# Where the gain and bias of the mixers' norms are applied, and what the residual and the MLP's sums then read

## The chip, the cores and the metric

One core of one Trainium2 chip runs the whole program in one launch. The metric is the device time of one execution in microseconds (us); the time of the kernel before is the median of three runs. A profile is one further execution, recorded by the hardware profiler.

## The reference

A decoder trunk of two layers on 1024 tokens of width 1024, all in float32. Layer 0 mixes tokens with a gated convolution, layer 1 with windowed attention. Around each mixer and each MLP stands a residual sum and a layer norm; a gated embedding of the token closes each layer:

```
x = layer_norm(ALPHA * x + mixer(x), mix_g, mix_b)        # the change is here
x = layer_norm(ALPHA * x + square(relu(x @ w_up)) @ w_down, mlp_g, mlp_b)
x = x + (p @ w_proj) * sigmoid(x @ w_gate)
layer_norm(x, g, b) = (x - mean(x)) * rsqrt(var(x) + 1e-5) * g + b
```

g and b are vectors over the 1024 features. The first norm's result is read twice: by the MLP's up product, which needs it transposed (features on the partitions), and by the residual of the second sum, which needs it with tokens on the partitions.

## The kernel before, in words

**Numbers.** Every float32 operand of a product is split into a high part (a cast to fp32r, by ScalarE, `xh`, `wh`) and a low part (value minus high, by VectorE, `xl`, `wl`); a product is three matmuls, high by high, high by low, low by high (`mm3`). All large products are done block-wise with seven instead of eight sub-products, for which sums and differences of the quarters of each operand are formed. For the up product the token side is cut into four quarters: features 0 to 511 or 512 to 1023 (q) by tokens 0 to 511 or 512 to 1023 (h), kept as `self.xT[q, h]`, each a high and a low tile of 128 x 4 x 512.

**Order of work.** The program is written as a list of operations; a planner (`Recorder.schedule`) simulates the engines with fixed costs, and issues each engine's instructions in the order that it finds. `nc.later(n)` lowers the priority of what stands in it by n places, `nc.slack` makes the planner take an operand as ready some ns later. `nc.either` leaves it to the planner whether VectorE or GpSimd (POOL) runs an instruction. Engines run in that order, strictly one after another. All instructions are issued from one line, L488, so that the profile is read by tiles and not by lines. Every DMA is issued by SP, in one queue.

**Buffers.** Tiles come from tagged slots in the order of the requests: `z` (4), `g` (4), `t` (5), `A` (9), `B` (8), `X` (8), `E` (4 double ones), `bo` (2), `v` (1), `cst` (1). PSUM has eight banks, which move between the tags `ps` (sums of products) and `tr` (transposes).

**The end of a mixer.** `mix_out` (layer 0) and `outputs` in `attention` (layer 1) multiply by the output weights, a group of token tiles at a time. `mixed` adds the residual on VectorE. When both halves of a tile of 128 tokens are done, `layer_norm` runs on it: `stats` (VectorE and three small instructions on POOL and VectorE), then for each half of 512 features a normalization on ScalarE (`z`), a multiplication by a row of g on VectorE and an addition of a row of b on VectorE or POOL. g and b are rows of 512 loaded to all partitions (tag `g`). `to_xT` transposes the result on TensorE, four 128 x 128 blocks to a bank, and splits the bank into `self.xT`: a cast by ScalarE and a subtraction by VectorE that read PSUM. The tile itself is stored to DRAM (`self.mid`), from where `residual` loads it late in the down product and multiplies it by ALPHA.

**The MLP's start.** `mlp` first runs the top-left products of five pairs of up columns (`EARLY`; 24 matmuls each), which need only quarters (0, 0) and (1, 0). Meanwhile `token_forms` builds the four sums from all quarters. Where only high and low parts are at hand, it adds both parts of each quarter: five VectorE instructions for the first two sums of a block of 128 features, three each for the third and the fourth. Then follow the 16 pairs of up columns, seven products of 12 matmuls each; their hidden values are combined by `keep` and stored. In between, `work` prepares weights for later stages.

Of the kernel before, what the change touches and what calls it, by code (L numbers as in the profile page):

```python
# [10 lines left out]
F32 = mybir.dt.float32  # L11
# [65 lines left out]
UP_WORK = {6: ("gate", 0), 10: ("gate", 1), 14: ("gate", 2), 16: ("gate", 3), 20: ("down", 0), 22: ("down", 1)}  # L77
HID_SLACK = 3000.0
# [442 lines left out]
class Emit:  # L521
# [259 lines left out]
    def to_xT(self, xt, t, raw=None, slack=SLACK):  # L781

        for q in range(2):
            pv = self.transpose4(self.blocks(xt[q]), slack).rearrange("p (a b) -> p a b", a=4)
            sl = (slice(None), slice(None), slice(t % 4 * P, (t % 4 + 1) * P))
            if raw and q == 0:
                self.nc.scalar.copy(raw[t // 4][sl], pv)
                if t >= 4:
                    continue
# [23 lines left out]
    def layer_norm(self, t, gb, spill=None, raw=None, sums=None):  # L813
# [3 lines left out]
        rs = self.stats(xt) if sums is None else self.row_stats(xt, sums)  # L817
        for q in range(2):
# [3 lines left out]
            (nc.vector if sums and t % 4 > 1 else nc.either).tensor_tensor(out=xt[q], in0=z, in1=gb[1][q], op=ALU.add)  # L822
        self.to_xT(xt, t, raw, LAST_SLACK[self.gates] if sums else SLACK)
# [27 lines left out]
    def setup(self):  # L851
        nc, d = self.nc, self.d
        cst = self.const("cst", (P, 256 + NT * 32 + 2 * NH), F32)
        self.cc, self.sums = cst[:, 0 : 32 + 64 + TAPS + 1], cst[:, 32 + 64 + TAPS + 1 :]
        self.ident = self.const("ident", (P, P), F32)
        self.mhalf = self.const("mhalf", (P, 32), F32)[:, 0:1]
# [26 lines left out]
    def conv(self):  # L883
# [15 lines left out]
        nc.sync.dma_start(self.ident, d["ident"])  # L899
        scr = {}  # L900
# [385 lines left out]
        with nc.after(exchange):  # L1286
            gb = self.load_row("g", d["mix_g"][0:1]), self.load_row("g", d["mix_b"][0:1])
            ws.add(*[d["w_out"][0, u] for u in range(2)])
            ws.pump()
# [17 lines left out]
        self.mix_out(d["w_out"], gb)  # L1307
# [25 lines left out]
    def mix_out(self, w, gb):  # L1333

        nc, ws = self.nc, self.ws
        self.raw = None
# [97 lines left out]
    def token_forms(self, tags):  # L1434
# [18 lines left out]
        raw = {}  # L1453
        b11r, b12r = [[v[:, k, :] for k in range(4)] for v in self.raw] if self.raw else (None, None)
        sub, add = ALU.subtract, ALU.add
        B = {k: [quarter(k + 4 * j, h) for j in range(2) for h in range(2)] for k in range(4)}

        for k, (b11, b12, b21, b22) in B.items():
            if self.raw:
                t1 = tt(b12r[k], b11r[k], sub, b12r[k])  # L1460
            else:
                t1 = tt(f(b12[0]), f(b11[0]), sub)
                lo = tt(f(b12[1]), f(b11[1]), sub)
                tt(t1, lo, add, t1)
            raw[k] = self.sb(tags[4])
            tt(f(b22[0]), t1, sub, raw[k])
            tt(raw[k], f(b22[1]), add, raw[k])
            for j, r in ((2, raw[k]), (1, t1)):
                forms[j][k] = two(tags[j])
                self.split(r, *forms[j][k])  # L1470
        for k, (b11, b12, b21, b22) in B.items():
            if self.raw:
                t3 = tt(raw[k], b11r[k], sub, b11r[k])
            else:
                t3 = tt(raw[k], f(b11[0]), sub)
                tt(t3, f(b11[1]), sub, t3)
            forms[3][k] = two(tags[3])
            self.split(t3, *forms[3][k])
        for k, (b11, b12, b21, b22) in B.items():
            t4 = tt(f(b21[0]), raw[k], sub)  # L1480
            tt(t4, f(b21[1]), add, t4)
# [4 lines left out]
    def mlp(self, i):  # L1486
# [54 lines left out]
        for f in pairs:  # L1541
# [99 lines left out]
    def down_seven(self, i, cs, start, end, rest):  # L1641
# [41 lines left out]
        def product(a, b, to, bank=None, own=(None, None), last=False, low=None, full=()):  # L1683
# [11 lines left out]
            for t in range(4 if last else 0):  # L1695
                with nc.later(LATE if to == [(0, 1)] else 0):
                    self.layer_norm(t + 4 * to[0][0], gb, None, self.raw, sums[t + 4 * to[0][0]])
# [217 lines left out]
    def attention(self):  # L1915
        nc, d, ws = self.nc, self.d, self.ws
        ac = self.sb("cst", n=256 + NT * 32 + 2 * NH)
# [99 lines left out]
        self.x, self.raw = [], None  # L2017
# [8 lines left out]
        gb = []  # L2026
        held = {}

        def outputs(cc, tiles, end, norm):
# [300 lines left out]
```

## Time and profile before

| | |
|---|---|
| median of 3 runs | 2104.5 us (2100.63 to 2106.58) |
| the profiled execution | 2101.52 us, of which its span is 2099.8 |
| TensorE (PE) busy | 2082.9 us, 99% |
| its weight loads (PEld) | 1729.3 us, 82% |
| VectorE (DVE) busy | 1700.9 us, 81% |
| ScalarE (ACT) busy | 1207.1 us, 57% |
| GpSimd (POOL) busy | 295.1 us, 14% |
| granted TensorE clock | 1.0 |
| end of layer 0's mixer, then its MLP's first products | from about 310 to 430 us |
| the same in layer 1 | from about 1365 to 1490 us |

How to read the rows. A row of the timeline gives the start in us, the time that it took, engine, operation, the tiles out<-in, shape and count, and in brackets the idle time of the engine before it and what ended it. A row of the windows gives the stretch, its length, then the busy time and number of instructions of PE, PEld, DVE, ACT and POOL, the granted clock, the DMA share and GB/s. A row of the groups ends in the busy time and the mean ns of one, then the engine's idle time before them and who ended it. Matmul records overlap each other: one of 512 columns lasts 0.39 us, and its distance to the next tells the rate.

### The profile page before, as it was taken

Reading aid. Unit: us, or ns where it says so; the run is one execution under the profiler, and the core shown is the slowest. Engines: PE = TensorE matmul, PEld = TensorE weight load, DVE = VectorE, ACT = ScalarE, POOL = GpSimd, SP = SyncE. Lnnn points to the kernel's source line nnn. Section 1 sums busy time; section 2 is a strip of 40 time slices with the busy share of each in tenths; the row PEclk is TensorE's granted clock in tenths of the full one; section 3 lists DMA queues with packets and bytes.
Section 4 is the critical chain, followed back from the end, with each engine's and each line's share of the span. In section 5 each row is a group of like instructions: output and inputs, shape, how many; then the busy total and the mean of one; then the engine's idle time right before and its main releaser. Section 6 shows DMA issues by size and latency. Waiting matters only on the chain.

```text
span 2099.8 us, 29286 instructions
## 1 busy us (share of the span) xinstructions
PE 2082.9 (99%) x9784; PEld 1729.3 (82%) x9784; DVE 1700.9 (81%) x2631; ACT 1207.1 (57%) x2224; POOL 295.1 (14%) x513
## 2 busy tenths in 40 slices
PE   9999999999999999999999999999999999999999
PEld 7888888888888888888888888877888888888877
DVE  8999789987876889987963587989787778888688
ACT  6777654766666644345742488656666563333374
POOL 0533114000000000002220265520000000000040
PEclk9999999999999999999999999999999999999999
DMA  6669864878776879875566877587878785575635
GB/s 226 192 202 296 294 197 143 298 265 273 269 270 216 307 257 319 279 262 215 171 211 192 319 227 238 188 298 249 269 259 275 254 285 200 181 247 171 233 126 191
DMA packets 239063, 502.01 MB, mean 239 GB/s; under 512 B 24128, under 2 KB 62784, under 8 KB 238912
## 3 DMA queue, kind: packets, MB, share of 16 engines
q1 hardware_dynamic: 238912, 500.14, 71.2%
q8 instruction: 77, 1.26, 0.2%
q14 instruction: 74, 0.61, 0.1%
HBM read 337.26 MB, written 160.17 MB: 237 GB/s over the span
## 4 chain that ended last, share of the span: by engine, by line
PE 88%; DVE 5%; DMA 3%; ACT 2%; issue 1%; POOL 1%; SPq 0%; DVEq 0%; ACTq 0%; POOLq 0%
PE ps L488 67%; PE tr L488 21%; DVE z L488 1%; DMA wh<-gate_t 1%; ACT z L488 1%; DVE g L488 1%; POOL sm L488 1%; DMA raw<-in_w_up_dram 1%; DVE wl L488 1%; DVE B L488 1%; DVE xl L488 0%; DVE t L488 0%; DVE v L488 0%; DVE sm L488 0%; DVE X L488 0%
## 5 line engine op out<-in xcount | busy, mean ns | idle before, releaser
L488 PE MATMUL ps<-xh,xl 128*128 128x512 f32 x618 | 240.5, 389 | 0.0
L488 PE MATMUL ps<-xl,xh 128*128 128x512 f32 x618 | 240.5, 389 | 0.0
L488 PE MATMUL ps<-xh 128*128 128x512 f32 x618 | 240.5, 389 | 0.0
L488 POOL TENSOR_SCALAR sm<-sm 128x1 f32<-128x1 f32 x72 | 26.8, 374 | 1362.9 <-DVE E L488 1200.1
L488 PE MATMUL ps<-xl,wh 128*128 128x512 f32 x536 | 210.3, 393 | 0.4 <-DVE xl L488 0.4
L488 PE MATMUL ps<-xh,wh 128*128 128x512 f32 x536 | 209.4, 393 | 0.8 <-DVE xl L488 0.5
L488 PE MATMUL ps<-xh,wl 128*128 128x512 f32 x536 | 210.0, 392 | 0.0
L488 ACT CAST wh<-raw 128x1024 fp32r<-128x1024 f32 (+2 forms) x130 | 115.5, 890 | 77.5 <-PE ps L488 47.9
L488 PE MATMUL ps<-wh,xh 128*128 128x512 f32 (+1 forms) x352 | 138.5, 395 | 3.2 <-DMA wh<-gate_t 1.2
L488 PE MATMUL ps<-wh,xl 128*128 128x512 f32 (+1 forms) x352 | 138.6, 394 | 0.1
L488 PE MATMUL ps<-wl,xh 128*128 128x512 f32 (+1 forms) x352 | 138.6, 394 | 0.0
L488 ACT CAST xh<-wh 128x1024 fp32r<-128x1024 f32 x76 | 79.7, 1049 | 99.7 <-PE ps L488 53.0
L488 PEld LDWEIGHTS ps<-xh 128*128 128x128 f32 x618 | 116.0, 188 | 24.2
L488 PEld LDWEIGHTS ps<-xh,xl 128*128 128x128 f32 x618 | 116.0, 188 | 24.1
L488 ACT CAST wh<-g 128x512 fp32r<-128x512 f32 x136 | 81.2, 618 | 94.9 <-PE ps L488 52.6
L488 PEld LDWEIGHTS ps<-xl,xh 128*128 128x128 f32 x618 | 116.1, 188 | 23.9
L488 DVE TENSOR_TENSOR wl<-raw,wh 128x1024 fp32r<-128x1024 f32 (+2 forms) x96 | 93.2, 972 | 37.0 <-ACT wh L488 35.8
L488 DVE TENSOR_TENSOR wl<-g,wh 128x512 fp32r<-128x512 f32 x136 | 90.9, 690 | 38.5 <-ACT wh L488 38.4
L488 PEld LDWEIGHTS ps<-xh,wh 128*128 128x128 f32 x536 | 100.9, 188 | 21.9 <-DVE xl L488 0.7
L488 PEld LDWEIGHTS ps<-xl,wh 128*128 128x128 f32 x536 | 101.0, 188 | 21.1 <-DVE xl L488 1.1
L488 PEld LDWEIGHTS ps<-xh,wl 128*128 128x128 f32 x536 | 100.9, 188 | 20.7
L488 ACT ACTIVATE t<-t 128x512 f32<-128x512 f32 x144 | 90.8, 632 | 34.9 <-DVE t L488 33.3
(406 smaller groups left out, 5644.6 us busy)
## 6 DMA issues: line engine op xcount, KB each, us to landing
wh<-hid SPq DMA_DIRECT2D x78, 512.0 KB, 4.6
raw<-in_w_up_dram SPq DMA_DIRECT2D x68, 512.0 KB, 4.3
wl<-in_w_down_dram SPq DMA_DIRECT2D x58, 512.0 KB, 5.3
hid<-zz SPq DMA_DIRECT2D x96, 256.0 KB, 4.8
hid<-t SPq DMA_DIRECT2D x64, 256.0 KB, 4.7
z<-in_w_dw_dram SPq DMA_DIRECT2D x56, 288.0 KB, 4.1
raw<-hid SPq DMA_DIRECT2D x30, 512.0 KB, 4.7
xh<-in_w_gate_dram SPq DMA_DIRECT2D x32, 256.0 KB, 5.6
```

What stands on the lines that cost most here:

```text
L488: getattr(getattr(nc, o.eng), o.name)(*a, **k)
```

## The change

The norm ahead of each MLP (`mix_norm` in place of `layer_norm`) now runs on a pair of token tiles. ScalarE normalizes in place, TensorE transposes the normalized values without g and b, four blocks (two feature blocks of the two tiles) to a bank, and ScalarE reads each half of the bank with the column of g as scale and the column of b as bias, since features stand on the partitions there: the layout that g and b need is a new input of 128 x 32 (`ln_cols`). The result is a float32 tile in SBUF (tag `t` for the first 512 tokens, one of two new whole quarters `self.raw` for the other 512), which is then split. Quarter q = 0 of the second half of the tokens is not split any more, since only the sums read it; the tiles `xh01` and `xl01` of the quarter that is unused hold the two whole quarters.

`token_forms` uses the two whole quarters: three instructions instead of five for the first two sums of a block.

What is stored for the residual is the normalized value without g and b. `affine` applies them later: after each of the 16 pairs of the up product one half tile is loaded from DRAM (tag `A`), multiplied by a row of g, added to a row of b (the rows in the slots `v` and `cst`), both on VectorE, and stored back. `layer_norm` stays for the second norm.

```diff
+AFFINE_BY = 200
...
-    def to_xT(self, xt, t, raw=None, slack=SLACK):
+    def to_xT(self, xt, t, raw, slack):
...
-    def layer_norm(self, t, gb, spill=None, raw=None, sums=None):
+    def layer_norm(self, t, gb, raw, sums):
...
-        if spill:
+    def mix_norm(self, ts, i):
+
+        nc, spill = self.nc, self.mid[i]
+        lg, lb = (self.cols[:, 16 * i + 8 * k : 16 * i + 8 * k + 8] for k in range(2))
+        if ts[0] == 4:
+            self.raw = tuple(nc.tile(f"x{p}01", (P, 4, HT), F32) for p in "hl")
+        h = ts[0] // 4
+        tok = slice(ts[0] % 4 * P, (ts[0] % 4 + 2) * P)
+        zs = [self.x[t] for t in ts]
+        for t, z in zip(ts, zs):
+            rs = self.stats(z)
             for q in range(2):
-                nc.sync.dma_start(spill[t][:, q * HT : (q + 1) * HT], xt[q])
+                nc.scalar.activation(z[q], z[q], AF.Identity, bias=rs[:, 1:2], scale=rs[:, 0:1])
+        for f in range(0, KB, 2):
+            q = f // 4
+            blk = [slice((f + j) % 4 * P, ((f + j) % 4 + 1) * P) for j in range(2)]
+            ps = self.transpose4([z[q][:, b] for b in blk for z in zs], SLACK)
+            if h:
+                y = self.raw[q][:, f % 4 : f % 4 + 2, tok]
+            else:
+                y = self.sb("t").rearrange("p (a b) -> p a b", a=2)
+            for j in range(2):
+                nc.scalar.activation(
+                    y[:, j, :], ps[:, 2 * j * P : 2 * (j + 1) * P], AF.Identity,
+                    bias=lb[:, f + j : f + j + 1], scale=lg[:, f + j : f + j + 1],
+                )
+            if (h, q) != (1, 0):
+                self.split(y, *[x[:, f % 4 : f % 4 + 2, tok] for x in self.xT[q, h]])
+        for t, z in zip(ts, zs):
+            for q in range(2):
+                nc.sync.dma_start(spill[t][:, q * HT : (q + 1) * HT], z[q])
+
+    def affine(self, i, k):
+
+        nc, d = self.nc, self.d
+        q, t = k // NT, k % NT
+        c = slice(q * HT, (q + 1) * HT)
+        if t == 0:
+            self.rows = [self.sb(v) for v in ("v", "cst")]
+            for v, w in zip(self.rows, ("mix_g", "mix_b")):
+                nc.sync.dma_start(v, d[w][i : i + 1, c].to_broadcast([P, HT]))
+        v = self.sb("A")
+        nc.sync.dma_start(v, self.mid[i][t][:, c])
+        for row, op in zip(self.rows, (ALU.mult, ALU.add)):
+            nc.vector.tensor_tensor(out=v, in0=v, in1=row, op=op)
+        nc.sync.dma_start(self.mid[i][t][:, c], v)
...
+        nc.sync.dma_start(self.cols, d["ln_cols"])
...
-                    if cc == 1:
-                        self.layer_norm(t, gb, self.mid[0])
+                if cc == 1:
+                    self.mix_norm(g, 0)
...
-        for k, (b11, b12, b21, b22) in B.items():
-            if self.raw:
-                t1 = tt(b12r[k], b11r[k], sub, b12r[k])
-            else:
-                t1 = tt(f(b12[0]), f(b11[0]), sub)
-                lo = tt(f(b12[1]), f(b11[1]), sub)
-                tt(t1, lo, add, t1)
-            raw[k] = self.sb(tags[4])
-            tt(f(b22[0]), t1, sub, raw[k])
-            tt(raw[k], f(b22[1]), add, raw[k])
+        for k in range(4):
+            t1, t2 = b12[k], b22[k]
+            for x in b11[k]:
+                tt(t1, f(x), sub, t1)
+            tt(t2, t1, sub, t2)
...
+            with nc.later(AFFINE_BY):
+                self.affine(i, f // 2)
...
-                if norm:
-                    self.layer_norm(t, gb, self.mid[1])
+                if norm and t % 2:
+                    self.mix_norm((t - 1, t), 1)
```

The planner makes a new order for the whole program out of this. The engines' queues hold as many TensorE instructions as before (9784 matmuls, transposes among them), 4 fewer on VectorE, 56 more on ScalarE, 20 fewer on POOL and 65 more DMAs on SP. Two places show what moves.

The first is TensorE at the end of layer 1's mixer, where the last pair of token tiles (6 and 7; their halves are in four tiles B) is transposed among the top-left products of the MLP. Before:

```order
L488 MATMUL ps_2546_14038<-xh_241_305,wh_2531_13959 128x512
L488 MATMUL ps_2542_14024<-ident_303,B_2263_12679 128x128 x4
L488 MATMUL ps_2546_14038<-xl_242_306,wh_2531_13959 128x512
L488 MATMUL ps_2546_14038<-xh_241_305,wl_2529_13954 128x512
L488 MATMUL ps_2548_14051<-ident_303,B_2273_12723 128x128 x4
L488 MATMUL ps_2549_14056<-ident_303,B_2407_13357 128x128 x4
L488 MATMUL ps_2562_14143<-ident_303,B_2438_13508 128x128 x4
L488 MATMUL ps_2567_14158<-xh_245_309,wh_2531_13959 128x512
```

And in the changed kernel, from the pair's first transpose on; 27 products stand between the pair's own last product and the first row, and B_2254 and B_2267 are the first token tile, B_2397 and B_2412 the second:

```order
L489 MATMUL tr_2538_14053<-ident_303,B_2254_12705 128x128
L489 MATMUL ps_2543_14071<-ident_303,B_2254_12705 128x128
L489 MATMUL ps_2522_13962<-xh_241_305,wh_2527_13989 128x512
L489 MATMUL ps_2522_13962<-xl_242_306,wh_2527_13989 128x512
L489 MATMUL tr_2545_14078<-ident_303,B_2267_12753 128x128
L489 MATMUL ps_2522_13962<-xh_241_305,wl_2526_13986 128x512
L489 MATMUL ps_2522_13962<-xh_241_305,wh_2527_13989 128x512
L489 MATMUL tr_2538_14053<-ident_303,B_2397_13347 128x128
L489 MATMUL tr_2538_14053<-ident_303,B_2254_12705 128x128
L489 MATMUL tr_2538_14053<-ident_303,B_2397_13347 128x128
```

A bank now takes blocks of both token tiles in turn, so that every bank but for its first blocks waits for the later tile, and the runs of four from one tile are broken up by products.

The second place is SP's queue in layer 0's up stage, about the third of its hidden chunks. Before, with stores of hidden values (hid), of prepared gate weights (gate) and loads of up weights (raw):

```order
L488 DMA hid_3_0_138_202<-t_1146_5507 128x512
L488 DMA hid_2_4_134_198<-zz_1153_5545 128x512
L488 DMA raw_1161_5620<-in_w_up_dram 128x1024
L488 DMA hid_2_5_135_199<-zz_1153_5545 128x512
L488 DMA hid_2_6_136_200<-z_1072_4964 128x512
```

And in the changed kernel, where A is the residual's half tile and mid its place in DRAM:

```order
L489 DMA A_1133_5507<-mid_0_108_172 128x512
L489 DMA gate_low_t_267_331<-xh_994_4512 128x512
L489 DMA xh_994_4512<-in_w_gate_dram 128x512 x2
L489 DMA hid_2_2_132_196<-t_1122_5439 128x512
L489 DMA hid_2_4_134_198<-zz_1139_5551 128x512
L489 DMA hid_3_0_138_202<-t_1134_5514 128x512
L489 DMA hid_2_5_135_199<-zz_1139_5551 128x512
L489 DMA hid_2_6_136_200<-z_1047_4911 128x512
L489 DMA raw_1149_5636<-in_w_up_dram 128x1024
L489 DMA xh_994_4512<-in_w_gate_dram 128x512
L489 DMA gate_t_260_324<-xl_1011_4625 128x512
L489 DMA mid_0_108_172<-A_1133_5507 128x512
```

Between the load of a half tile and its store back stand the stores and weight loads of about one pair.

More of the change, by code (lines that the diff above doesn't have):

```diff
@@ L821, in layer_norm @@
             nc.vector.tensor_tensor(out=z, in0=z, in1=gb[0][q], op=ALU.mult)
-            (nc.vector if sums and t % 4 > 1 else nc.either).tensor_tensor(out=xt[q], in0=z, in1=gb[1][q], op=ALU.add)
-        self.to_xT(xt, t, raw, LAST_SLACK[self.gates] if sums else SLACK)
-        if spill:
-            for q in range(2):
-                nc.sync.dma_start(spill[t][:, q * HT : (q + 1) * HT], xt[q])
+            (nc.vector if t % 4 > 1 else nc.either).tensor_tensor(out=xt[q], in0=z, in1=gb[1][q], op=ALU.add)
@@ L2310, in layout @@
         r[k + "_b"] = c(np.asarray(a[k + "_ln_b"]))
+    r["ln_cols"] = c(np.concatenate([cm(np.asarray(a[k][i])) for i in range(2) for k in ("mix_ln_g", "mix_ln_b")], axis=1))
     wu = np.asarray(a["mlp_w_up"])
```

46 lines of the change are left out of this document (20 added, 26 removed).

## The prediction

> **What bounds the kernel now.** I read the page first, then TensorE's rows in order of time, then the stages in the windows, then the places in the two stages that the change touches where TensorE stands. The page says how full each engine is:
>
> ```profile
> span 2099.8 us, 29286 instructions
> PE 2082.9 (99%) x9784; PEld 1729.3 (82%) x9784; DVE 1700.9 (81%) x2631; ACT 1207.1 (57%) x2224; POOL 295.1 (14%) x513
> PEclk9999999999999999999999999999999999999999
> ```
>
> TensorE is busy 99% at the full clock all through. Busy alone does not say that it runs at its rate, so the next rows, TensorE's own in order of time, are needed:
>
> ```profile
> 358.92 0.39 PE L488 MATMUL ps<-wl,xh 128*128 128x512 f32 x1
> 359.15 0.39 PE L488 MATMUL ps<-wh,xl 128*128 128x512 f32 x1
> 359.38 0.40 PE L488 MATMUL ps<-wh,xh 128*128 128x512 f32 x1
> 359.61 0.60 PE L488 MATMUL tr<-ident,B 128*128 128x128 f32 x4
> 359.96 0.48 PE L488 MATMUL ps<-wl,xh 128*128 128x512 f32 x1
> 360.28 0.39 PE L488 MATMUL ps<-wh,xl 128*128 128x512 f32 x1
> ```
>
> Each 128x512 product starts 0.23 us after the one before. Four transposes and the product behind them take 360.28 - 359.61 = 0.67, so a transpose costs (0.67 - 0.23) / 4 = 0.11. Below I count a wait as the step between two starts minus 0.23 a product and 0.11 a transpose. By stage (columns: PE, PEld, DVE, ACT, POOL busy, granted clock, DMA share, GB/s):
>
> ```profile
> 360.00:430.00 70.00, 70.00 (x325) 58.10 (x324) 65.56 (x106) 49.78 (x85) 6.62 (x8) 1.00 0.78 270
> 500.00:700.00 200.00, 200.00 (x884) 165.61 (x883) 149.38 (x224) 125.90 (x211) 0.00 (x0) 1.00 0.77 264
> 1365.00:1420.00 55.00, 53.27 (x248) 43.54 (x247) 48.44 (x79) 30.53 (x48) 13.95 (x14) 1.00 0.85 300
> 1420.00:1490.00 70.00, 68.10 (x295) 54.68 (x294) 62.32 (x102) 44.25 (x79) 0.00 (x0) 1.00 0.73 243
> sum 2100.00, PE 2082.87 PEld 1729.28 DVE 1700.88 ACT 1207.11 POOL 295.07; mean PE 148.78 PEld 123.52 DVE 121.49 ACT 86.22 POOL 21.08
> ```
>
> Layer 0's norm and sums (360 to 430) and the up stage (500 to 700) leave TensorE no idle time at all. Layer 1's norm (1365 to 1420) leaves 1.73 us, its sums and the first up pairs (1420 to 1490) 1.90. The whole program has 17.1. The change can win only what TensorE waits, and nearly all of that in its reach lies in layer 1.
>
> **The change part by part.** *TensorE's work:* the program has the same products and the same 128 transposes for the two norms; only their order moves. Priced at nothing; six more runs of transposes at the 0.09 by which a run lengthens the product behind it (0.48 against 0.39) would be 0.5 at most.
>
> *The norm without a multiplication and an addition ahead of the transposes.* This is the place where TensorE waits for the last pair of layer 1:
>
> ```profile
> 1390.24 0.39 PE L488 MATMUL tr<-xh,wh 128*128 128x512 f32 x1
> ...
> 1399.77 0.60 PE L488 MATMUL ps<-ident,B 128*128 128x128 f32 x4
> 1400.13 0.48 PE L488 MATMUL ps<-xl,wh 128*128 128x512 f32 x1
> 1400.45 0.40 PE L488 MATMUL ps<-xh,wl 128*128 128x512 f32 x1
> 1401.07 0.66 PE L488 MATMUL ps<-ident,B 128*128 128x128 f32 x4 [0.22 <-POOL B L488]
> 1402.74 1.27 PE L488 MATMUL ps<-ident,B 128*128 128x128 f32 x8 [1.02 <-POOL B L488]
> 1404.50 0.50 PE L488 MATMUL ps<-xh,wh 128*128 128x512 f32 x1 [0.48 <-DVE xl L488]
> ```
>
> From 1399.77 to 1404.50 are 4.73 us, which hold 16 transposes (1.76) and two products (0.46): 2.5 us of waiting, for POOL's addition of b and then for a PSUM bank that the late transposes fill. The engines that feed them, at the same time:
>
> ```profile
> 1395.36 1.52 ACT L488 ACTIVATE z<-B,sm 128x512 f32<-128x512 f32 x2 [0.70 <-DVE sm L488]
> ...
> 1397.49 2.38 DVE L488 TENSOR_TENSOR z<-z,g 128x512 f32<-128x512 f32 x2
> 1397.72 0.82 ACT L488 ACTIVATE z<-B,sm 128x512 f32<-128x512 f32 x1
> 1398.44 0.80 ACT L488 ACTIVATE v<-B,sm 128x512 f32<-128x512 f32 x1
> 1399.35 3.33 POOL L488 TENSOR_TENSOR B<-z,g 128x512 f32<-128x512 f32 x2 [0.63 <-DVE z L488]
> ```
>
> With the change the transposes read what ScalarE writes; the 2.38 and the 3.33 leave the path. What is late next is ScalarE: its second tile is done at 1398.54 and 1399.24, that is 8.3 and 9.0 us after the sums of that pair were finished (1390.24). In the changed order TensorE comes to that tile's transposes 31 products and 3 transposes after the same point, 31 x 0.23 + 0.33 = 7.4 us. So 0.9 would still be waited if ScalarE were no sooner, and nothing if it gains the 0.9 from the freed VectorE and from a weight split that no longer stands between the four normalizations. I take 0.5: the gain is 2.5 - 0.5 = 2.0, between 1.6 and 2.5. The first tile is in time (27 x 0.23 = 6.2 us after 1390.24 for the first half, which ScalarE had done at about 1396.1 even in the old chain), and the last pair's splits have the five top-left products behind them, 5 x 24 x 0.23 = 27 us of cover. Beside POOL's additions VectorE takes 1.19 for one of its multiplications (2.38 for two), so it gains more than the instructions that leave. The Trainium skill, "SBUF — State Buffer", section Who interferes with whom, states that a VectorE instruction with two SBUF inputs contends with a GpSimd one that reads SBUF; this trace agrees. The same section says that a DMA contends with no compute engine; by it the transfers added below could only be late themselves, and slow no engine.
>
> In layer 0 the same chain costs TensorE nothing (70.00 of 70.00), so its removal is worth nothing there.
>
> *The sums for the MLP.* With two quarters whole, the first sums need 12 instead of 20 VectorE instructions, splits apart, ahead of the products that use them.
>
> ```profile
> 1426.86 0.62 PE L488 MATMUL tr<-X,wh 128*128 128x512 f32 x2
> 1427.87 0.50 PE L488 MATMUL tr<-X,wh 128*128 128x512 f32 x1 [0.40 <-DVE X L488]
> 1428.67 0.40 PE L488 MATMUL tr<-X,wl 128*128 128x512 f32 x1
> 1429.13 1.01 PE L488 MATMUL ps<-E,wh 128*128 128x512 f32 x2
> ...
> 1409.00:1420.00 11.00, 11.00 (x50) 9.12 (x49) 11.00 (x20) 6.79 (x13) 0.00 (x0) 1.00 0.75 256
> L488 DVE TENSOR_TENSOR xh<-xh 128x512 f32<-128x512 f32 x48 | 32.1, 683 | 0.1
> ```
>
> VectorE is full there (11.00 of 11.00), and eight fewer at 0.68 are 5.5 us. The waits for X (1427.87 - 1426.86 - 2 x 0.23 = 0.55) and E (0.23) go: 0.8. Bounds 0 and 0.8, nearer to the second because 5.5 is far more than is missing. What is late next is the weight of the E products, which comes from a DMA: the two in the last TensorE row take 1.01 against 0.62 of two in the first. I leave that 0.39.
>
> *g and b for the residual, in the up stage.* A layer gets 16 loads, 32 VectorE instructions and 16 stores of 256 KB, in steps of one half tile a pair.
>
> ```profile
> sum 330.00, PE 329.81 PEld 272.79 DVE 257.17 ACT 213.44 POOL 0.00; mean PE 29.98 PEld 24.80 DVE 23.38 ACT 19.40 POOL 0.00
> 480.00:510.00 30.00, 30.00 (x135) 24.82 (x134) 25.57 (x40) 21.46 (x37) 0.00 (x0) 1.00 0.86 294
> A<-mid SPq DMA_DIRECT2D x16, 256.0 KB, 5.2
> ...
> 1486.87 0.39 PE L488 MATMUL tr<-xl,wh 128*128 128x512 f32 x1
> 1488.42 0.73 PE L488 MATMUL ps<-A,wh 128*128 128x512 f32 x2 [1.16 <-ACT t L488]
> ```
>
> The first row sums eleven windows from 390 to 720: VectorE is idle 72.8 us, and 32 x 0.68 = 21.8 fit, so they cost nothing; without that cover they would cost at most 21.8 a layer. A pair of up columns takes 7 x 12 x 0.23 = 19 us, so the 8.4 MB of transfers spread over 16 x 19 = 304 us, 28 GB/s; by the busiest window (0.86 at 294) that is 0.08 of share, to 0.94. A load lands in 5.2 us, far less than a pair. What can suffer is whoever stands behind these transfers in SP's queue: weight loads and the stores of the hidden tiles, whose buffers ScalarE waits for. The last two rows show such a late copy: 1488.42 - 1486.87 - 0.23 = 1.3 us. I take 0, with 1.3 each as the price of one; a gain is excluded, since nothing is taken off SP in that stage.
>
> *The column constants at the start* add one SP issue of about 0.4 us ahead of the second half's x; 0, at most 0.4. *The planner's other moves:* the order also shifts in the convolution and in attention without any change of work there. I take 0 and keep 2 either way.
>
> Sum: -2.0 - 0.8 = -2.8 us. The profiled execution took 2101.52 (span 2099.8 and 1.7 around it), so a like one would take 2098.7. The median of the runs is 3.0 higher, 2104.5, and my forecast for it is 2101.7, which is -0.13%. A measurement of this kernel can tell about 0.3%, 6.3 us, from no change, so this counts as no change.
>
> **The rivals.** *ScalarE becomes the bound.* It takes over the affine: eight 128x256 instructions a pair.
>
> ```profile
> 266.89 1.48 ACT L488 ACTIVATE t<-tr,cst 128x256 f32<-128x256 f32 x3 [0.64 <-PE tr L488]
> ...
> 365.00:376.00 11.00, 11.00 (x55) 9.16 (x54) 9.37 (x16) 9.69 (x18) 4.05 (x4) 1.00 0.79 269
> 376.00:387.00 11.00, 11.00 (x54) 9.12 (x53) 9.27 (x16) 7.47 (x12) 0.00 (x0) 1.00 1.04 384
> ```
>
> The same instruction stands in the convolution's norm at 1.48 / 3 = 0.49, so 3.9 a pair: 9.69 + 3.9 is 2.6 over the 11 us of a pair, and the next window's 3.5 of idle takes it up. If it is not taken up, 2.6 a layer, 5.2 in all, reach TensorE: 2101.7 + 5.2 = 2106.9. For it: the busy window; against: one quarter is no longer split at all, and 27 us of cover. The Trainium skill, "ScalarE: Activation LUTs", section Rules for kernel authors, says to do multiplications and additions on VectorE, not on ScalarE, which speaks against this change; by that rule this rival would be the likeliest. The rows bear it out only so far that ScalarE is tight for one window: chance 0.10.
>
> *Slower: SP's queue and the stores in the up stage.* In-order SP holds an affine store until VectorE is done, the stores behind it land later, ScalarE's copies wait for their buffers and TensorE for the copies, 1.3 us each. It exceeds 0.3% if it hits 7 of the 32 pairs: 7 x 1.3 - 2.8 = 6.3. At 11 pairs: 14.3 - 2.8 = +11.5, 2116.0. For it: a share of up to 0.94. Against: 200.00 of 200.00 with the gates' weight work already in the same queue. 0.10.
>
> *Faster: every wait in the touched stages goes and the new order is better elsewhere.* 2.5 + 0.8 + 0.39, and 1.3 at 1488, make 5.0; with 2 from elsewhere 7.0: 2097.5. For it: in the changed order the first up products of layer 1 are no longer cut up among each other. 0.17.
>
> **How the numbers follow.** The forecast has 0.63, with a range of its own from 2098 to 2106; the rivals 0.10, 0.10 and 0.17. Over 0.3% faster (below 2098.2): 0.17 and 0.03 of the forecast's edge, 0.20. Over 0.3% slower (above 2110.8): 0.10 and 0.02, 0.12. The rest, 0.68, is no change. From 2095, which takes in the faster case with the waits of both layers, to 2110, which takes in ScalarE's and the first of SP's, lie about 0.85.
>
> **What would show it.** Right: at the end of layer 1's mixing no row waits for POOL, under 1 us is left between the transposes of the last pair, the first X product waits for nobody; DVE in the up stage goes up by some 20 us a layer and PE stays full. Wrong: TensorE rows in the up stage that wait for ACT copies or for wh or wl; waits for ACT xh or xl behind the transposes; or a gain of over 6 us, which could not come from these stages alone.

## The result: slower, and not by a wait

The changed kernel took 2115.6 us (median of 4 runs, 2113.1 to 2119.0) against 2103.6 for the kernel before beside it (2100.6 to 2106.6): a ratio of 1.0058, 95% interval 1.0038 to 1.0079. The forecast was 2101.7. The profiled execution has a span of 2113.8 us, 14.0 more than that of before.

From the page after: the span and the busy time, and three groups of products (columns: busy time, mean ns of one, idle time before them).

```profile
span 2113.8 us, 29443 instructions
PE 2099.5 (99%) x9784; PEld 1731.4 (82%) x9784; DVE 1685.0 (80%) x2627; ACT 1230.3 (58%) x2280; POOL 257.8 (12%) x493
...
L489 PE MATMUL ps<-xl,xh 128*128 128x512 f32 x636 | 247.7, 390 | 0.0
...
L489 PE MATMUL ps<-xl,wh 128*128 128x512 f32 x588 | 234.5, 399 | 0.2 <-DVE xl L489 0.2
...
L489 PE MATMUL ps<-wh,xl 128*128 128x512 f32 x448 | 178.4, 398 | 0.0
```

The same groups on the page of before:

```profile
L488 PE MATMUL ps<-xl,xh 128*128 128x512 f32 x618 | 240.5, 389 | 0.0
...
L488 PE MATMUL ps<-xl,wh 128*128 128x512 f32 x536 | 210.3, 393 | 0.4 <-DVE xl L488 0.4
...
L488 PE MATMUL ps<-wh,xl 128*128 128x512 f32 (+1 forms) x352 | 138.6, 394 | 0.1
```

VectorE and POOL work less, ScalarE a little more, and TensorE has 16.6 us more of busy time for the same 9784 matmuls. A product of xl and xh, whose operands both lie in the tiles of the token quarters, costs what it did. A product of such a tile and a weight slot (xl, wh, in either role) costs 4 to 6 ns more, although hardly any of them waits. The windows that answer to those of the prediction:

```profile
360.00:430.00 70.00, 70.00 (x322) 57.31 (x321) 57.43 (x94) 55.85 (x97) 2.95 (x8) 1.00 0.89 311
500.00:700.00 200.00, 200.00 (x873) 163.65 (x872) 153.06 (x236) 119.88 (x203) 0.00 (x0) 1.00 0.80 272
1365.00:1420.00 55.00, 55.00 (x260) 44.65 (x258) 35.18 (x62) 36.99 (x63) 3.28 (x8) 1.00 0.96 334
1420.00:1490.00 70.00, 70.00 (x306) 57.31 (x306) 65.01 (x107) 45.56 (x81) 0.00 (x0) 1.00 0.85 287
```

Everywhere in the reach of the change TensorE is now full; the 1.73 and the 1.90 us of idle time in layer 1 are gone. But in 500 to 700, which was full before too, 200.00 us hold 873 matmuls where they held 884: 229.1 ns each instead of 226.2, at the same granted clock of 1.00. "Full" was no proof of the same rate. Which products are the slow ones is seen in the groups of that stretch by form, first before, then after (the first tile is the moving operand, the second the stationary one; A and E are forms, that is sums of quarters):

```profile
L488 PE MATMUL ps<-xl,wh 128*128 128x512 f32 x101 | 39.3, 389 | 0.0
...
L488 PE MATMUL ps<-A,wl 128*128 128x512 f32 x40 | 15.6, 389 | 0.0
```

```profile
L489 PE MATMUL ps<-xl,wh 128*128 128x512 f32 x87 | 34.5, 396 | 0.0
...
L489 PE MATMUL ps<-E,wl 128*128 128x512 f32 x35 | 13.6, 389 | 0.0
...
L489 PE MATMUL ps<-A,wl 128*128 128x512 f32 x28 | 10.9, 390 | 0.0
```

With the same weight slots, a plain quarter costs 7 ns more and a form costs nothing more. The timeline has it too. After, in layer 1's up stage:

```profile
1485.68 0.62 PE L489 MATMUL tr<-X,wh 128*128 128x512 f32 x2
...
1486.82 0.40 PE L489 MATMUL ps<-xh,wh 128*128 128x512 f32 x1
...
1488.22 0.40 PE L489 MATMUL ps<-xh,wh 128*128 128x512 f32 x1
...
1489.62 0.63 PE L489 MATMUL ps<-B,wh 128*128 128x512 f32 x2
```

Five products with X take 1486.82 - 1485.68 = 1.14 us, 228 ns each; the twelve with xh and xl take 1489.62 - 1486.82 = 2.80, 233 ns each, and none waits.

The distance from each product's start to the next start, its step, was counted over the whole trace. Beyond 226.5 ns a product, the steps of 200 to 260 ns hold 7.0 us before and 25.3 after: +18.3. The rest, with 226.5 ns taken off for a product and 0.11 us for a transpose (waits, a lower clock, the start and the end), is 36.8 before and 32.5 after: -4.3. Together that is the 14.0. Of the steps of 200 to 260 ns, 759 of 8182 are over 230 ns before and 3369 of 8186 after.

What the two groups of operands differ in is where they lie. The change also resized constants, which stand in each partition right ahead of the token quarters:

```diff
-        cst = self.const("cst", (P, 256 + NT * 32 + 2 * NH), F32)
+        cst = self.const("cst", (P, 256 + NT * 32 + NH), F32)
         self.ident = self.const("ident", (P, P), F32)
-        self.mhalf = self.const("mhalf", (P, 32), F32)[:, 0:1]
+        cols = self.const("cols", (P, 40), F32)
```

Before, they take 2176 + 512 + 128 = 2816 bytes, after, 2112 + 512 + 160 = 2784. So the eight tiles of the quarters begin 32 bytes lower, at byte 163680 instead of 163712, while the weight slots and forms ahead of the constants stay. Every size before was such that all operands of the large products began 128 bytes past a multiple of 256. After, the quarters begin 96 past one.

### The profile page after: what moved, and what is told of

The parts are those of the page before. It is cut to its first block, busy times and chain, and to the rows that moved or that the text cites. A ratio compares the mean times of both kernels' runs of the same rounds, so it can differ in the third digit from the quotient of the medians.

```text
span 2113.8 us, 29443 instructions
## 1 busy us (share of the span) xinstructions
PE 2099.5 (99%) x9784; PEld 1731.4 (82%) x9784; DVE 1685.0 (80%) x2627; ACT 1230.3 (58%) x2280; POOL 257.8 (12%) x493
## 4 chain that ended last, share of the span: by engine, by line
PE 92%; DMA 2%; DVE 2%; ACT 1%; issue 1%; POOL 1%; SPq 0%; DVEq 0%; POOLq 0%; ACTq 0%
PE ps L489 75%; PE tr L489 17%; POOL sm L489 1%; ACT z L489 1%; DMA B<-scr 0%; DVE g L489 0%; DMA raw<-in_w_kv_dram 0%; DVE E L489 0%; DMA z<-in_w_dw_dram 0%; DMA wh<-hid 0%; DVE xl L489 0%; DMA wl<-gate_low_t 0%; DMA wh<-gate_t 0%; DVE t L489 0%; DMA X<-in_xT_dram 0%
## 5 line engine op out<-in xcount | busy, mean ns | idle before, releaser
L489 PE MATMUL ps<-xl,wh 128*128 128x512 f32 x588 | 234.5, 399 | 0.2 <-DVE xl L489 0.2
L489 PE MATMUL ps<-xh,wh 128*128 128x512 f32 x588 | 233.9, 399 | 0.2 <-ACT xh L489 0.2
L489 PE MATMUL ps<-xh,wl 128*128 128x512 f32 x588 | 234.1, 398 | 0.0
L489 PE MATMUL ps<-wh,xh 128*128 128x512 f32 x448 | 179.5, 401 | 3.0 <-DVE xh L489 1.5
L489 PE MATMUL ps<-wl,xh 128*128 128x512 f32 x448 | 178.9, 400 | 0.0
L489 PE MATMUL ps<-wh,xl 128*128 128x512 f32 x448 | 178.4, 398 | 0.0
L489 PEld LDWEIGHTS ps<-xh,wh 128*128 128x128 f32 x588 | 111.0, 189 | 25.1 <-ACT xh L489 0.7
L489 PEld LDWEIGHTS ps<-xh,wl 128*128 128x128 f32 x588 | 110.7, 188 | 25.3
L489 PEld LDWEIGHTS ps<-xl,wh 128*128 128x128 f32 x588 | 111.0, 189 | 24.8 <-DVE xl L489 0.5
L489 DVE TENSOR_TENSOR xl<-wh,xh 128x1024 fp32r<-128x1024 f32 x76 | 92.8, 1222 | 26.0 <-ACT xh L489 23.6
```

What stands on the lines that cost most here:

```text
L489: getattr(getattr(nc, o.eng), o.name)(*a, **k)
```

## The experiments

Theory 1: the step of a product depends on where its operands begin, one against the other, and the change lost 18 us by that alone. Theory 2, the rival: the added work (the residual's transfers, VectorE's multiplications and additions, ScalarE's scaling) takes something from TensorE in the stages where it runs.

### The change with its quarters where they stood

```diff
-        cst = self.const("cst", (P, 256 + NT * 32 + NH), F32)
         self.ident = self.const("ident", (P, P), F32)
-        cols = self.const("cols", (P, 40), F32)
+        cst = self.const("cst", (P, 256 + NT * 32 + NH), F32)
+        cols = self.const("cols", (P, 48), F32)
```

> The changed kernel whole, its instructions in the same order; only the sizes and the order of three constants differ (ident first, cols 48 columns wide where it had 40), so that the eight x quarters stand again where they stood in the kernel before (byte 163712 of each partition, a multiple of 128, where the change had put them at 163680). Theory 1, placement: a 128x512 product starts its successor about 233.3 ns later, where it is 226.7 ns otherwise, if its moving and its stationary operand stand at different places within 128 bytes; in the change 3369 products are over 230 ns against 759 before, which costs 18.3 us. Then this run is 2115.6 - 18.3 = 2097 us (2095 to 2100), with some 760 products over 230 ns. Theory 2, the moved work: the residual's 16 loads and stores per MLP and DVE's 20 us more per layer take memory bandwidth from TensorE. Then nothing changes: 2113 to 2119 us and some 3370 products over 230 ns.

Measured: 2096.4 us (10 runs, 2094.7 to 2098.9), ratio to before 0.9971, interval 0.9962 to 0.9981; 715 products over 230 ns. That is 19.1 us less than the change as made (18.3 by the two ratios to before, since the two were measured on different occasions), by eight columns that nobody reads and a new order of three constants. Its groups and its window, to be read beside the two above:

```profile
L489 PE MATMUL ps<-xl,wh 128*128 128x512 f32 x85 | 33.1, 389 | 0.0
...
L489 PE MATMUL ps<-A,wl 128*128 128x512 f32 x28 | 10.9, 389 | 0.0
```

```profile
500.00:700.00 200.00, 200.00 (x884) 165.58 (x884) 153.64 (x234) 123.02 (x207) 0.00 (x0) 1.00 0.83 283
```

389 for quarter and form alike, and 884 in 200 us again, with all the added work in place. Theory 2 is out. This version beats both kernels. The new order also moves `ident`, the operand of the transposes, which stood 128 bytes away from most of their other operands, modulo 256, and now stands at the same place. That gains nothing: one transpose behind another steps at 109 ns in both.

### The kernel before with its quarters moved

Three kernels with no other instruction in them, and one in which everything moves together:

```diff
-        self.mhalf = self.const("mhalf", (P, 32), F32)[:, 0:1]
+        self.mhalf = self.const("mhalf", (P, 24), F32)[:, 0:1]
```

> The kernel before, with one constant 24 columns wide where it had 32: the eight x quarters stand 32 bytes lower (96 within 128, all weight slots and forms still at 0); no instruction differs. Theory 1, placement: as in the change some 3370 products over 230 ns, 18 us more: 2122 us (2117 to 2126). Theory 2, the moved work: no change, 2101 to 2107 us and some 760 products over 230 ns.

```diff
+        self.mhalf = self.const("mhalf", (P, 16), F32)[:, 0:1]
```

> The kernel before, with that constant 16 columns wide: the x quarters stand 64 bytes lower (64 within 128). Theory 1 in the form that every difference within 128 bytes counts: 2122 us as with 32 bytes. Theory 1 in the form that only a place that is no multiple of 64 bytes counts: 2103.5 us, some 760 products over 230 ns. Theory 2, the moved work: 2103.5 us.

```diff
+        pad = self.const("pad", (P, 24), F32)
+        nc.gpsimd.memset(pad[:, 0:1], 0.0)
         for tag, n in SLOTS.items():
```

> The kernel before, with 96 bytes of unused memory ahead of everything: every tile that TensorE reads stands at 96 within 128 (and one memset of 128x1 is added on GpSimd at the start). Theory 1 as the difference between the two operands: all pairs stand alike, 2103.5 us, some 760 products over 230 ns. Theory 1 as each operand's own place: all of some 8200 products take 6.6 ns more, 54 us: 2158 us. Theory 2, the moved work: 2103.5 us.

| quarters against weight slots | time, us | ratio to before (95%) | products over 230 ns |
|---|---|---|---|
| 32 bytes lower | 2119.5 | 1.0079 (1.0064 to 1.0093) | 3523 |
| 64 bytes lower | 2114.9 | 1.0061 (1.0047 to 1.0075) | 2867 |
| 128 bytes lower (below) | 2117.1 | 1.0065 (1.0048 to 1.0082) | 2441 |
| all 96 bytes higher | 2103.4 | 1.0004 (0.9995 to 1.0013) | 743 |

The first loses 16.6 us without the change (18.9 in its steps of 200 to 260 ns). The last shows that moving all operands by the same 96 bytes costs nothing: what counts is the difference. At 64 bytes the time lies between the 2122 and the 2103.5 that were expected, and the two directions part: with the quarter moving and the slot stationary (quarter 64 lower) the mean step is 233.3 ns, with the roles exchanged 229.4. So a multiple of 64 is not enough.

### The products alone

Series of 192 products with the operands at chosen places, in a program that does nothing else meanwhile.

> Not the kernel but its product alone: 17 series of 192 128x512 products, nothing else running, four stationary and two moving tiles in turn; in each series the moving operand begins m and the stationary operand s bytes past a multiple of 128 (m or s from 0, 16, 32, 64, 96, 128). It computes nothing of the reference. Theory 1 as the difference between the two operands: 226.5 ns a product where m and s are alike (0 and 0, 32 and 32, 64 and 64, 96 and 96, 128 and 0, 0 and 128), about 233 where they differ by 32 or 96; by the third experiment's rows 233 for m 64 against s 0 and 229 for m 0 against s 64. Rival, the difference matters only while VectorE, ScalarE and DMAs use the memory too: 226.5 in every series, so that the price in the kernel is one of contention.

Groups by form (the name gives the bytes past a multiple of 128 of the moving and the stationary operand):

```profile
L43 PE MATMUL mov32B_sta0B<-x,w 128*128 128x512 f32 x192 | 45.0, 395 | 0.0
...
L43 PE MATMUL mov0B_sta64B<-x,w 128*128 128x512 f32 x192 | 45.0, 395 | 0.0
L43 PE MATMUL mov0B_sta128B<-x,w 128*128 128x512 f32 x192 | 45.0, 395 | 0.0
...
L43 PE MATMUL mov64B_sta0B<-x,w 128*128 128x512 f32 x192 | 44.1, 391 | 0.0
L43 PE MATMUL mov64B_sta64B<-x,w 128*128 128x512 f32 x192 | 43.7, 389 | 0.0
L43 PE MATMUL mov32B_sta32B<-x,w 128*128 128x512 f32 x192 | 43.7, 389 | 0.0
```

The column of 389 to 395 is the length of a record; the step from start to start moves with it. Steps: 226.67 ns at equal places, 233.3 at 32 against 0, 0 against 32, 64 against 32 and others. The rival, contention with other traffic, falls: nothing else runs here. (The first series begins at 427 ns a product; behind its first eight it has 228.6 on the mean, and it repeats as 226.67 at the end.) Two of my figures were wrong. With the moving operand 64 ahead a product takes 228.9 and not 233: in the kernel the quarter stood 64 bytes lower, so that a moving quarter was behind and a moving weight slot ahead, and I had taken lower for higher. And 128 bytes apart, which I expected to be free, cost 232 to 233. So a second set of places, and the kernel before with its quarters 128 bytes lower:

> The product alone again, 21 series of 192 as in the series before, at other places; it computes nothing of the reference. The first such run gave 226.67 ns where both operands stood alike, 232 to 233 where they differed by 128 bytes in either direction, and 228.9 with the moving operand 64 bytes ahead. If the difference counts within 256 bytes: 226.67 at 128 and 128, and where m or s is 256 or 512; 233 at 0 and 128, 384 and 0, 0 and 384; 192 and 0 like 0 and 64 (233), 0 and 192 and 320 and 0 like 64 and 0 (229). If it counts within 512 bytes: 256 and 0 and 0 and 256 are slow too, 233. If it counts within 128 bytes and the 233 of the first run was something else: 226.67 at every multiple of 128.

```profile
L43 PE MATMUL mov192B_sta0B<-x,w 128*128 128x512 f32 x192 | 45.0, 395 | 0.0
L43 PE MATMUL mov0B_sta128B<-x,w 128*128 128x512 f32 x192 | 45.0, 395 | 0.0
...
L43 PE MATMUL mov64B_sta0B<-x,w 128*128 128x512 f32 x192 | 44.1, 391 | 0.0
L43 PE MATMUL mov0B_sta192B<-x,w 128*128 128x512 f32 x192 | 44.1, 391 | 0.0
...
L43 PE MATMUL mov128B_sta128B<-x,w 128*128 128x512 f32 x192 | 43.7, 389 | 0.0
L43 PE MATMUL mov256B_sta0B<-x,w 128*128 128x512 f32 x192 | 43.7, 389 | 0.0
L43 PE MATMUL mov0B_sta512B<-x,w 128*128 128x512 f32 x192 | 43.7, 389 | 0.0
```

> The kernel before with its constants made 128 bytes smaller in all (unused columns of two constants; ident stands first), so that the x quarters stand 128 bytes lower against the weight slots and the forms; no instruction differs. If the difference of the two operands counts within 256 bytes, as the products alone say: as with 32 and 64 bytes, 2115 to 2120 us and some 3000 or more products over 230 ns. If it counts within 128 bytes alone: 2103 us and some 760. If nothing of the placement counted: 2103 us.

The difference counts within 256 bytes, as the first case of each expectation had it: 226.67 ns at differences of 0, 256 and 512, 228.9 with the moving operand 64 ahead (or 192 behind), and about 231 to 237 at every other difference tried, down to 4 bytes (236.7 and 232.4). The kernel moved by 128 took 2117.1, as that case had it, but with 2441 products over 230 ns where some 3000 or more were expected: its products of a quarter and something else step at 232.7 on the mean, but a third of them at 228 to 230.

Which read meets which was tried with one product in eight out of place:

> The product alone, four series of 192 with every operand at a multiple of 256 bytes, except that every eighth product has its stationary operand, its moving operand, or both 32 bytes further; it computes nothing of the reference. If a product's own two operands collide: the step behind the eighth product is slow (about 233) with one operand moved, and no step is slow with both. If the moving read of a product collides with the weight load of the next one: with the stationary moved the step behind the seventh is slow, with the moving operand moved the step behind the eighth, and with both moved two steps of eight are slow.

Neither held. With only the stationary operand of every eighth product moved, the step ahead of that product is the first slow one (235.0), but the three steps behind it are slow too (228.3, 232.3, 231.0), and a moved moving operand slows six of eight. The records do not show the load of the moved weights beside the first slow step: they put it 0.69 to 0.50 us ahead of the start of its product, beside a step of 227 ns. With both moved five of eight steps are slow, so it is not a matter of the product's own pair alone. How the two reads meet stays open.

The Trainium skill, "TensorE: Matmul & The Clock Gate", section Step-by-step: what each phase is for, says that loading the next weights takes no SBUF read bandwidth from the running matmul, since the two have read ports of their own. At a difference of 0 nothing here speaks against it. At others a product takes 2 to 10 ns longer, by where its stationary operand lies against the moving one, so the sentence cannot be relied on at every placement and the measurement decides; that it is the loading that takes this time is not shown.

### The parts of the change, with the quarters in place

The residual's g and b left out of the up stages:

```diff
-            with nc.later(AFFINE_BY):
-                self.affine(i, f // 2)
```

> The padded change without the step that applies g and b to the residual in the up stages: 32 loads, 64 VectorE instructions and 32 stores of 256 KB fewer. It leaves out g and b of the residual that the down stage adds. As the prediction has it, that step costs nothing: 2096.4 us (2095 to 2099), and TensorE without waits in both up stages as in the padded change. Rival, its transfers and VectorE's work cost time that the padded change still pays: 2 to 7 us less, 2089 to 2094 us.

Measured: 2096.5 us, 0.9971 (0.9960 to 0.9983), as with it. The whole time alone would not settle it, since the plan differs elsewhere too. The up stage of layer 0 does, first with the step, then without:

```profile
390.00:720.00 330.00, 330.00 (x1458) 273.23 (x1457) 262.15 (x400) 209.08 (x352) 0.00 (x0) 1.00 0.84 290
390.00:720.00 330.00, 330.00 (x1458) 273.15 (x1457) 248.05 (x376) 209.45 (x352) 0.00 (x0) 1.00 0.77 268
```

TensorE runs 1458 matmuls in 330.00 us in both, and in layer 1, from 1480 to 1700, 972 in 220.00 us in both. The step costs nothing. That also fits the Trainium skill, "SBUF — State Buffer", section SBUF: two separate sides, by which transfers and engines do not slow each other.

The norm undone, the shorter sums kept (again without `affine`, which it does not need):

```diff
-                nc.scalar.activation(z[q], z[q], AF.Identity, bias=rs[:, 1:2], scale=rs[:, 0:1])
+                v = self.sb("z")
+                nc.scalar.activation(v, z[q], AF.Identity, bias=rs[:, 1:2], scale=rs[:, 0:1])
+                nc.vector.tensor_tensor(out=v, in0=v, in1=gb[0][q], op=ALU.mult)
+                nc.either.tensor_tensor(out=z[q], in0=v, in1=gb[1][q], op=ALU.add)
...
+                nc.scalar.copy(y[:, j, :], ps[:, 2 * j * P : 2 * (j + 1) * P])
```

> The padded change with one part undone: g and b as rows ahead of the transposes, by VectorE and by VectorE or GpSimd, as in the kernel before; the banks are copied out without them and the residual needs nothing more. Kept are the pairs, the two whole quarters and the shorter sums. As the prediction has it, the norm is what gains in layer 1: the waits for GpSimd at the end of layer 1's mixing come back, 1.6 to 2.5 us, and the time is 2098 to 2100 us. Rival, the gain came from the sums and from the order of the instructions alone: no wait for GpSimd's addition there and 2096.4 us.

Measured: 2104.1 us, 1.0003 (0.9994 to 1.0012). TensorE at the end of layer 1's mixing, where the waits for POOL's addition are back:

```profile
1403.38 0.33 PE L489 MATMUL tr<-ident,B 128*128 128x128 f32 x1 [0.20 <-POOL B L489]
1405.05 0.87 PE L489 MATMUL ps<-ident,B 128*128 128x128 f32 x6 [1.34 <-POOL B L489]
1406.66 0.33 PE L489 MATMUL ps<-ident,B 128*128 128x128 f32 x1 [0.74 <-ACT xh L489]
```

2.3 us of idle time stand there, 2.9 by the steps; the prediction had 2.5 by the steps in the kernel before. But the whole came out at 7.6 over the run without `affine`, not at the 1.6 to 2.5 that were expected. Three waits in attention are back as well (1276 to 1285), which the padded change has not. They are shown here as they stand in the kernel before:

```profile
1273.41 0.50 PE L488 MATMUL ps<-A,v 128*128 128x512 f32 x1 [0.28 <-DVE A L488]
1280.67 0.50 PE L488 MATMUL ps<-A,bo 128*128 128x512 f32 x1 [0.37 <-ACT A L488]
1282.78 0.50 PE L488 MATMUL ps<-A,bo 128*128 128x512 f32 x1 [0.24 <-POOL A L488]
```

By the steps they cost 1.4 us. A further 1.9 is a wait for a bank copy of ScalarE's in layer 0 (from 369.7 to 371.8) that this mixture alone has. That makes 6.2 of the 7.6, and the rest is not traced. So the 7.6 are an upper figure for the norm.

The other part undone, all quarters split and the sums made the long way:

> The padded change with its other part undone: all four quarters are split as they leave the banks, none is kept whole, and the sums for the MLP are made from the splits by the longer sequence of the kernel before (20 VectorE instructions where the change has 12, splits apart). The norm stays as changed: g and b as the banks are read, the residual in the up stage. As the prediction has it, the sums are worth 0.8 us, in layer 1 alone: waits for X and E come back ahead of the first sum products there, 0.3 to 1.2 us, none in layer 0, and the time is 2097 to 2098 us. Rival, the sums are what takes VectorE and ScalarE off TensorE's path after the norm: waits of 3 us or more over the two layers and 2099.5 us or more.

Its edit puts the `token_forms` of the kernel before in place of the new one, and in `mix_norm`:

```diff
-        if ts[0] == 4:
-            self.raw = tuple(nc.tile(f"x{p}01", (P, 4, HT), F32) for p in "hl")
+        self.raw = None
...
-            if h:
-                y = self.raw[q][:, f % 4 : f % 4 + 2, tok]
-            else:
-                y = self.sb("t").rearrange("p (a b) -> p a b", a=2)
+            y = self.sb("t").rearrange("p (a b) -> p a b", a=2)
...
-            if (h, q) != (1, 0):
-                self.split(y, *[x[:, f % 4 : f % 4 + 2, tok] for x in self.xT[q, h]])
+            self.split(y, *[x[:, f % 4 : f % 4 + 2, tok] for x in self.xT[q, h]])
```

Measured: 2101.6 us, 0.9992 (0.9982 to 1.0002), 5.1 more than the padded change. TensorE ahead of the sum products of layer 1, then a wait in layer 0's norm:

```profile
1427.73 0.39 PE L489 MATMUL ps<-X,wl 128*128 128x512 f32 x1
1429.26 0.74 PE L489 MATMUL ps<-X,wh 128*128 128x512 f32 x2 [1.15 <-ACT X L489]
```

```profile
379.35 0.50 PE L489 MATMUL ps<-wh,wh 128*128 128x512 f32 x1 [0.59 <-ACT t L489]
```

With two more at 1506 and 1525 (0.59 and 0.39 by the steps, for ScalarE's copies t) that is about 3.0 us: the rival's size, spread over both layers, not 0.8 in one. All of these waits end with ScalarE, which in this mixture also copies and casts the quarter that the change leaves unsplit, so they are not the price of the eight VectorE instructions alone. The other 2 of the 5.1 are not traced. The two parts do not add up (7.6 and 5.1 against 6.5 for the change in place): each mixture is planned anew and has waits that neither kernel has.

## Why the prediction was wrong

**The step that failed** is the first one: "the program has the same products and the same 128 transposes for the two norms; only their order moves. Priced at nothing". The number of products was right. Their duration was taken from before's rows, 0.23 us, as if it were a property of the shape. 3318 of 8186 products are of a quarter and something outside the quarters; their mean step went to 233.2 ns, and the whole loss in the steps is 18.3 us. No row of the trace of before could show this, since there the two operands of every such product differ by a multiple of 256 bytes. The code could have raised the question: the resized constants stand in the diff, ahead of the most used operands, and I priced only the transfer that fills them.

**The norm** was right in mechanism: no row waits for POOL at the end of layer 1's mixing, and nothing is idle there. In the changed kernel, ScalarE's normalizations of the last pair, then TensorE at the pair's first transpose, at the second tile's first and at the last ones:

```profile
1409.61 2.93 ACT L489 ACTIVATE B<-B,sm 128x512 f32<-128x512 f32 x4
...
1412.25 0.27 PE L489 MATMUL tr<-ident,B 128*128 128x128 f32 x1
...
1413.51 0.49 PE L489 MATMUL tr<-ident,B 128*128 128x128 f32 x3
...
1415.90 0.60 PE L489 MATMUL tr<-ident,B 128*128 128x128 f32 x4
1416.26 0.48 PE L489 MATMUL ps<-xl,wh 128*128 128x512 f32 x1
```

ScalarE is done at 1412.54, 6.6 us after the pair's sums (27 products ahead of 1412.25) where it took 9.0, and TensorE comes to the second tile at 1413.51. So the 0.5 that I left for a late ScalarE is not there, and the gain was 2.5, not 2.0. (The 1.19 for a multiplication beside POOL's addition was a mean of two unlike ones: the first of the two takes 1.78 us, beside the addition, the second 0.68.) What I missed is attention's 1.4. It belongs to this part, since those waits come back with the old norm and not with the old sums; but no norm runs yet where they stand, so it is the planner's order there, or a slot, and which of them no run tells.

**The sums** were right in layer 1 as far as the rows go (the first sum products wait for nobody after). The 0.8 may be undersized: without this part some 3 us of waits come back over both layers, but they end with ScalarE and not, as the prediction had it, with a full VectorE.

**The residual** at nothing was right, with the cover that was named. VectorE's rise was not: for 390 to 720 I expected some 20 us more and the change shows 261.73 against 257.17, with 13 instructions more in the stretch where I had counted 32; eight leave it with the sums, the others are not traced. Between the padded change with and without the step it is 262.15 against 248.05, for 24 instructions. "A gain is excluded" was wrong as well: the wait of 1.3 us at 1488, in layer 1's up stage, is gone (from 1480 to 1700 TensorE is busy 220.00 of 220.00 us, before 218.84). It comes with the new plan; a wait of 0.59 stands near this place in the run with the split sums.

**The planner's other moves**, kept at 2 either way, cost 1.2 at the end of the convolution's norm. Before, seven products stand between the first transposes there and the next; after, one, and TensorE waits four times (0.83, 0.30, 0.39 and 1.53 idle; before 0.91 and 1.02):

```profile
262.74 0.47 PE L489 MATMUL ps<-wh,wl 128*128 128x512 f32 x1
264.05 0.55 PE L489 MATMUL tr<-ident,X 128*128 128x128 f32 x3 [0.83 <-DVE X L489]
...
265.22 0.55 PE L489 MATMUL tr<-ident,A 128*128 128x128 f32 x3 [0.30 <-POOL A L489]
266.16 0.66 PE L489 MATMUL tr<-ident,A 128*128 128x128 f32 x4 [0.39 <-ACT t L489]
...
268.80 0.53 PE L489 MATMUL ps<-wh,xh 128*128 128x512 f32 x1 [1.53 <-DVE xh L489]
```

Behind these waits the granted clock fell to half for 3.4 us in this execution (0.89 in the window from 265 to 280), some 1.6 us more. In the padded change, with the same waits, it did not, and with the split sums it did for 6.8 us. In the profiled executions the padded change is 4.9 us shorter than before (2094.9 against 2099.8); the terms named here, 2.5, 0.8, 1.3 and 1.4 gained and 1.2 lost, make 4.8, and smaller waits elsewhere go both ways.

**The rivals.** The slower one gave 2116.0 and the time was 2115.6, by chance: its mechanism, stores late in SP's queue and TensorE waiting for copies in the up stage, is absent (200.00 of 200.00, and no change without `affine`). A time that fits is no evidence for the cause; the rows that were to show the cause are not there. ScalarE did not become the bound either. The faster rival, at 2097.5, is near what the change does once its operands are back in place, 2096.4, but only half of it holds: the waits in the touched stages do go (but for one of 0.70 us in layer 1, at 1458.77), while elsewhere the new order gains 1.4 and loses 1.2, not the 2 that it was given.

## What to carry to other kernels

Where TensorE is the bound, count the matmuls in a full window, not only the idle time: the same rate is a claim of its own. A diff that changes the size of any buffer moves every buffer behind it, so look where the operands of the large products begin against each other, and pad what stands ahead of them so that the differences stay. Before a change is judged by its time, compare it with the same change at the old addresses: here the verdict went from 0.58% slower to 0.29% faster.

## What the runs showed of the hardware

A stream of 128x512 fp32r products, each with new weights, steps at 226.67 ns where the moving and the stationary operand begin a multiple of 256 bytes apart in their partitions, at 228.9 where the moving one is 64 bytes ahead, and at some 231 to 237 at the other differences tried (4, 8, 16, 32, 96 and 128 bytes, and 64 or 192 the slow way round), with no other engine at work. Where both operands share an offset (32, 64, 96 and 128 were tried) it is 226.67. One product in eight out of place slows several of its neighbours (four steps of 228 to 235 with only its stationary operand moved). A transpose does not mind: most of them stand 128 bytes from `ident` in the kernel before, 64 in the change and 0 in the padded change, and one behind another steps at 109 ns in all three. Why it is so, no run here shows.
